# Splitting the first weight tile and turning the two token halves of four norms separately in a two-layer encoder kernel

## The chip, the cores and the metric

The kernel runs on one core of a Trainium2 chip. The metric is the device time of one execution in microseconds (us). The engines are named as in the profile: PE is TensorE, DVE is VectorE, ACT is ScalarE, POOL is GpSimd, SP is SyncE, which here issues the DMAs.

## What is computed

Two layers over 256 tokens of 1024 features. Each layer is a mixer (five groups of heads on one input projection, then an output projection) and a feed-forward part with product-key experts (PEER). Both begin with an RMS norm:

```python
def rmsnorm(x, g):
    xf = x.astype(jnp.float32)
    xf = xf * lax.rsqrt(jnp.mean(xf * xf, axis=-1, keepdims=True) + EPS)
    return xf.astype(x.dtype) * g

for l in range(DEPTH):
    xn = rmsnorm(x, norm_mix[l])
    proj = xn @ w_in[l]
    ...
    kv = rmsnorm(mem, mem_g) @ w_kv
    ...
    x = x + cat @ w_out[l]
    x = x + peer_ffn(rmsnorm(x, norm_ffn[l]), peer_wq[l], peer_subkeys[l], peer_u[l], peer_v[l])
```

mem is a second input of 256 rows of 1024 features; it feeds keys and values of one of the five groups.

## The kernel before

**Weights.** All weights come as a stream of 128 x 1024 tiles (class Stream). `fill` loads a tile w_raw by a DMA from SP (L70; three buffers) and splits it into w_hi, a rounded copy made by ACT (L82), and w_lo, the remainder made by DVE (L84), three buffers of each. A product is then three matmuls on a 128 x 128 block of weights: w_hi with the activations' high part (L240), w_hi with their low part (L241) and w_lo with the high part (L242). `out_t_job` runs them for the eight chunks of 128 features, each over all 256 tokens, into ps_mm; `pair_job` does so for two weight tiles in a row.

**Start.** The first products are those of mem with the four tiles of w_kv. `mem_load` brings mem in four pieces of two chunks each (L302) and splits each chunk into mh (ACT, L303) and ml (DVE, L304). Of the first two weight tiles the first is loaded ahead of the first memory piece and the second ahead of the second piece.

**Norms.** `rms_transposed` (L202 to L234) is called four times: for the mixer (into tile xs) and the feed-forward part (FFN; its scaled tokens lie in a tile named H) of either layer. The tokens lie on the partitions, in two halves of 128 (tt). Per half, ACT squares and sums (two instructions, L214), DVE makes the mean (L217), POOL the power -1/2 (L219), then DVE scales the first 512 features (L220) and ACT the others (L221). The matmuls need features on the partitions, so PE transposes (L227): a tile ps_t of PSUM takes two chunks of features with both halves, four transposes. ACT writes xh from it (L230, one instruction per chunk, 128 x 256), times the gain, and DVE writes xl (L231), which needs ps_t and xh. After the fourth chunk, `stream.release` lets the splitting of the next weights go on.

**Order.** The program is written as loops, but a scheduler of the framework sets the order of the instructions on each engine, by dependencies and priorities; `high_priority` surrounds the norms. On the chip each engine then runs its instructions in that order. In the mixer norms other work of the memory group is woven in: mm_vz (L478, ACT, from ps_v), rs_e (L364, ACT), ps_rb (L368, PE), mm_k (L417, DVE), mm_kz (L672, ACT). ps_t and ps_v share two buffers of PSUM there.

Of the kernel before, what the change touches and what calls it, by code (L numbers as in the profile page):

```python
# [10 lines left out]
F32 = mybir.dt.float32  # L11
# [4 lines left out]
AF = mybir.ActivationFunctionType  # L16
ALU = mybir.AluOpType
# [3 lines left out]
P = 128  # L21
T = 256
D = 1024
NC = D // P
# [6 lines left out]
AFTER = 3  # L31
MEM_CHUNK = 2
# [23 lines left out]
class Stream:  # L56


    def __init__(self, tc, raw_pool, hl_pool, sources, ahead, split_ahead):
        self.tc, self.nc, self.raw_pool, self.hl_pool, self.sources = tc, tc.nc, raw_pool, hl_pool, sources  # L60
        self.ahead, self.split_ahead = ahead, split_ahead
        self.raw, self.parts = {}, {}
        self.n_raw = self.n_parts = self.pos = 0
        self.limit = len(sources)
        self.after = ()

    def fill(self, upto=None):
        while self.n_raw < min(len(self.sources), self.pos + self.ahead, upto or len(self.sources)):
            t = self.raw_pool.tile([P, D], F32, name="w_raw")
            self.last_load = self.nc.sync.dma_start(t, self.sources[self.n_raw][0])  # L70
            self.raw[self.n_raw] = t
            self.n_raw += 1
        while self.n_parts < min(self.n_raw, self.pos + self.split_ahead, self.limit):
            r = self.raw.pop(self.n_parts)
            with ExitStack() as ctx:
                ctx.enter_context(self.tc.high_priority(SPLIT_AHEAD))
                for ins in self.after:
                    ctx.enter_context(self.tc.issue_after(ins.ins))
                self.after = ()
                hi = self.hl_pool.tile([P, D], F32R, name="w_hi")  # L80
                lo = self.hl_pool.tile([P, D], F32R, name="w_lo")
                self.nc.scalar.copy(hi, r)  # L82
                on_pool = self.sources[self.n_parts][1]
                (self.nc.gpsimd if on_pool else self.nc.vector).tensor_sub(lo, r, hi.bitcast(F32))  # L84
            self.parts[self.n_parts] = (hi, lo)
            self.n_parts += 1

    def release(self, after):

        self.limit, self.after = len(self.sources), after  # L90
# [46 lines left out]
def build(tc, x, mem, w_in, w_kv, w_out, wq, u_t, v_t, subk, pool_w, conv_pw, vec, dist, inv_count, ind, out, depth=2,  # L137
          dbg=None):
    nc = tc.nc
    V, A, G = nc.vector, nc.scalar, nc.gpsimd  # L140
# [14 lines left out]
    with (  # L155
# [9 lines left out]
        stream = Stream(tc, raw_pool, hl_pool, sources, 4, 3)  # L165
        ident = cp.tile([P, P], F32, name="ident")
# [23 lines left out]
        def vv(name, src=None):  # L190
            a, b = VEC[name]
            return (vecs if src is None else src)[:, a:b]
# [9 lines left out]
        def rms_transposed(pool, psum, src, xs, gain, hi, lo, in_hi=False):  # L202


            with tc.high_priority():
                for tt in range(2):
                    s = xs[:, tt, :]
                    ss = xp.tile([P, 2], F32, name="rn_ss", bufs=2)
                    for hf in range(2):
                        if in_hi:  # L210
                            junk = hi[:, 4 * tt + 2 * hf:4 * tt + 2 * hf + 2, :].rearrange("p c t -> p (c t)")
                        else:
                            junk = s[:, hf * 512:(hf + 1) * 512]
                        A.activation(junk, src[:, tt, hf * 512:(hf + 1) * 512], AF.Square, scale=1.0 / 32,  # L214
                                     accum_out=ss[:, hf:hf + 1])
                    ms = xp.tile([P, 1], F32, name="rn_ms", bufs=2)
                    V.tensor_scalar(ms, ss[:, 0:1], ss[:, 1:2], EPS, op0=ALU.add, op1=ALU.add)  # L217
                    rs = xp.tile([P, 1], F32, name="rn_rs", bufs=2)
                    pows.append(G.tensor_tensor(out=rs, in0=ms, in1=mhalf, op=ALU.pow))  # L219
                    V.tensor_scalar(s[:, 0:512], src[:, tt, 0:512], rs[:, 0:1], None, op0=ALU.mult)  # L220
                    A.activation(s[:, 512:], src[:, tt, 512:], AF.Identity, scale=rs[:, 0:1])  # L221
                for c in range(NC):
                    if c % 2 == 0:
                        ps = psum([P, 2, T], "ps_t")
                        for k in range(2):
                            for tt in range(2):
                                nc.tensor.transpose(ps[:, k, tt * P:(tt + 1) * P], xs[:, tt, (c + k) * P:(c + k + 1) * P],  # L227
                                                    ident)
                    pf = ps[:, c % 2, :]
                    a_ins = A.activation(hi[:, c, :], pf, AF.Identity, scale=gain[:, c:c + 1])  # L230
                    v_ins = V.scalar_tensor_tensor(lo[:, c, :], pf, gain[:, c:c + 1], hi[:, c, :].bitcast(F32),  # L231
                                                   op0=ALU.mult, op1=ALU.subtract)
                    if c == AFTER:
                        stream.release((a_ins, v_ins))  # L234

        def out_t_job(ps, hi, lo, xh, xl):

            for c in range(NC):
                wh, wl = hi[:, c * P:(c + 1) * P], lo[:, c * P:(c + 1) * P]
                nc.tensor.matmul(ps, wh, xh[:, c, :], start=(c == 0), stop=False)  # L240
                nc.tensor.matmul(ps, wh, xl[:, c, :], start=False, stop=False)  # L241
                nc.tensor.matmul(ps, wl, xh[:, c, :], start=False, stop=(c == NC - 1))  # L242
# [49 lines left out]
        def mem_load(mem_t, gains, weights=()):  # L292

            mh = xp.tile([P, NC, T], F32R, name="mh", tag="xh")
            ml = xp.tile([P, NC, T], F32R, name="ml", tag="xl")
            gain = vv("mem_norm", gains)
            with tc.high_priority() if not weights else nullcontext():
                for c in range(NC):
                    if c % MEM_CHUNK == 0:
                        if c // MEM_CHUNK in weights:  # L300
                            stream.fill(weights[c // MEM_CHUNK])
                        nc.sync.dma_start(mem_t[:, c:c + MEM_CHUNK, :], mem[:, c:c + MEM_CHUNK, :])  # L302
                    A.activation(mh[:, c, :], mem_t[:, c, :], AF.Identity, scale=gain[:, c:c + 1])  # L303
                    V.scalar_tensor_tensor(ml[:, c, :], mem_t[:, c, :], gain[:, c:c + 1], mh[:, c, :].bitcast(F32),  # L304
                                           op0=ALU.mult, op1=ALU.subtract)
            mem_parts[:] = [mh, ml]
# [779 lines left out]
```

## Time and profile before

| | us |
|---|---|
| runs shown | 2001.5, 2002.0, 2003.91 |
| median of the runs | 2002.0 |
| the profiled execution's own time | 2001.33 |
| its span in the trace | 1999.6 |
| PE busy in the span | 1964.6 (98%) |
| DVE busy | 1445.5 (72%) |
| ACT busy | 987.9 (49%) |

The span is the time from the first to the last instruction of the profiled execution; what the execution's own time has on top of it is start and end. Times in the trace count from the span's start. "Busy" sums the instructions' durations on an engine. The idle time before an instruction is shown in brackets with what released it: `[0.58 <-DVE xl L231]` means that the engine stood idle for 0.58 us until DVE's instruction on line 231, which writes xl, had ended.

### The profile page before, as it was taken

The numbers are of one execution on the slowest core, as the hardware profiler recorded it, in microseconds if no ns is written. First come the engines' busy times: TensorE is split into PE (matmuls) and PEld (weight loads), VectorE is DVE, ScalarE is ACT, GpSimd is POOL, SyncE is SP. The second block draws the span as 40 slices with busy tenths as digits, with TensorE's granted clock in tenths as the row PEclk, the third lists the DMA queues.
The fourth block names the chain that finished last, engine by engine and source line by source line (L and its number), as shares of the span: only waits on it lengthen the run. The fifth ranks groups of instructions, "written<-read, shape, count | busy, mean of one in ns | idle before, by whom it ended". The sixth has DMA issues, their size and how long they took to land.

```text
span 1999.6 us, 33683 instructions
## 1 busy us (share of the span) xinstructions
PE 1964.6 (98%) x13122; PEld 1809.9 (91%) x13122; DVE 1445.5 (72%) x2847; ACT 987.9 (49%) x1436; POOL 88.2 (4%) x141
## 2 busy tenths in 40 slices
PE   8999999999999999999999999999999999999999
PEld 7978999999999888888899789999999998888887
DVE  6976899788985655555578669987889755555555
ACT  6564455544444544444465645544444444444443
POOL 2310000000000000000023100000000000000000
PEclk9999999999999999999999999999999999999999
DMA  6314454434345555555553244554343455555554
GB/s 216 137 69 169 165 180 169 159 138 144 132 159 186 202 191 190 190 193 193 192 175 117 74 169 169 171 179 148 138 145 131 158 180 192 193 192 190 190 192 156
DMA packets 92769, 331.50 MB, mean 166 GB/s; under 512 B 10817, under 2 KB 11713, under 8 KB 92353
## 3 DMA queue, kind: packets, MB, share of 16 engines
q1 hardware_dynamic: 92608, 329.34, 48.3%
q8 instruction: 103, 1.69, 0.3%
q14 instruction: 58, 0.47, 0.1%
HBM read 328.25 MB, written 1.05 MB: 165 GB/s over the span
## 4 chain that ended last, share of the span: by engine, by line
PE 94%; DVE 3%; ACT 1%; issue 1%; DMA 0%; POOL 0%; SPq 0%; DVEq 0%; ACTq 0%; POOLq 0%
PE ps_mm L241 16%; PE ps_mm L240 16%; PE ps_mm L242 16%; PE acc_v L270 12%; PE acc_v L273 12%; PE acc_v L269 12%; PE ps_g L916 6%; PE ps_sc L804 1%; PE acc_o L269 1%; PE acc_o L273 1%; PE ps_o L496 1%; PE acc_o L270 1%; PE ps_ms L355 1%; DVE w_lo L84 1%; PE ps_t L227 0%
## 5 line engine op out<-in xcount | busy, mean ns | idle before, releaser
L84 DVE TENSOR_TENSOR w_lo<-w_raw,w_hi 128x1024 fp32r<-128x1024 f32 x612 | 748.6, 1223 | 421.2 <-ACT w_hi L82 420.9
L82 ACT CAST w_hi<-w_raw 128x1024 fp32r<-128x1024 f32 x612 | 641.6, 1049 | 760.3 <-PE ps_mm L241 499.4
L240 PE MATMUL ps_mm<-xh,w_hi 128*128 128x256 f32 x2624 | 752.5, 288 | 0.4 <-ACT xh L230 0.3
L241 PE MATMUL ps_mm<-xl,w_hi 128*128 128x256 f32 x2624 | 745.8, 285 | 0.1
L242 PE MATMUL ps_mm<-xh,w_lo 128*128 128x256 f32 x2624 | 744.4, 284 | 0.0
L241 PEld LDWEIGHTS ps_mm<-xl,w_hi 128*128 128x128 f32 x2624 | 505.5, 193 | 0.9 <-DVE xl L231 0.6
L240 PEld LDWEIGHTS ps_mm<-xh,w_hi 128*128 128x128 f32 x2624 | 504.3, 193 | 1.5 <-ACT xh L230 1.1
L242 PEld LDWEIGHTS ps_mm<-xh,w_lo 128*128 128x128 f32 x2624 | 504.8, 192 | 0.1
L270 PE MATMUL acc_v<-w_lo,a_hi 128*128 128x512 f32 x1016 | 316.3, 392 | 0.0
L273 PE MATMUL acc_v<-w_hi,a_lo 128*128 128x512 f32 x1016 | 315.2, 392 | 0.0
L269 PE MATMUL acc_v<-w_hi,a_hi 128*128 128x512 f32 x1016 | 273.9, 391 | 0.0
L273 PEld LDWEIGHTS acc_v<-w_hi,a_lo 128*128 128x128 f32 x1016 | 190.8, 188 | 42.4
L269 PEld LDWEIGHTS acc_v<-w_hi,a_hi 128*128 128x128 f32 x1016 | 190.8, 188 | 41.9
L270 PEld LDWEIGHTS acc_v<-w_lo,a_hi 128*128 128x128 f32 x1016 | 190.8, 188 | 40.7
L954 ACT CAST a_hi<-H 128x512 fp32r<-128x512 f32 x128 | 79.4, 622 | 153.7 <-PE acc_v L270 150.1
L956 DVE TENSOR_TENSOR a_lo<-H,a_hi 128x512 fp32r<-128x512 f32 x128 | 88.6, 693 | 77.7 <-ACT a_hi L954 77.7
L906 DVE TENSOR_SCALAR ag<-iota_f,i1T,gT 128x128 f32<-128x128 f32 x512 | 142.6, 342 | 0.0
L916 PE MATMUL ps_g<-ag,a 128*128 128x128 f32 x1024 | 125.1, 275 | 0.0
L916 PEld LDWEIGHTS ps_g<-ag,a 128*128 128x128 f32 x1024 | 120.2, 192 | 0.0
L901 DVE TENSOR_TENSOR a<-iota_f,i2T 128x1024 f32<-128x1024 f32 x64 | 77.8, 1218 | 1.7 <-PE ps_g L916 1.7
L921 DVE TENSOR_TENSOR H<-ps_g,H 128x184 f32<-128x184 f32 (+31 forms) x128 | 58.9, 464 | 1.2 <-ACT H L920 1.2
L943 ACT ACTIVATE H<-ps_mm 128x512 f32<-128x512 f32 (+31 forms) x106 | 49.4, 466 | 0.1
(242 smaller groups left out, 1296.7 us busy)
## 6 DMA issues: line engine op xcount, KB each, us to landing
w_raw<-u_t SPq DMA_DIRECT2D x256, 512.0 KB, 3.3
w_raw<-v_t SPq DMA_DIRECT2D x256, 512.0 KB, 3.4
w_raw<-w_in SPq DMA_DIRECT2D x40, 512.0 KB, 3.3
w_raw<-wq SPq DMA_DIRECT2D x32, 512.0 KB, 3.3
w_raw<-w_out SPq DMA_DIRECT2D x20, 512.0 KB, 3.2
w_raw<-w_kv SPq DMA_DIRECT2D x8, 512.0 KB, 3.4
H<-subk SPq DMA_DIRECT2D x2, 1024.0 KB, 4.9
mem_t<-mem SPq DMA_DIRECT2D x4, 256.0 KB, 6.2
```

The source lines that it names most:

```text
L82: self.nc.scalar.copy(hi, r)
L84: (self.nc.gpsimd if on_pool else self.nc.vector).tensor_sub(lo, r, hi.bitcast(F32))
L240: nc.tensor.matmul(ps, wh, xh[:, c, :], start=(c == 0), stop=False)
L241: nc.tensor.matmul(ps, wh, xl[:, c, :], start=False, stop=False)
L242: nc.tensor.matmul(ps, wl, xh[:, c, :], start=False, stop=(c == NC - 1))
L269: nc.tensor.matmul(accs[tt][hf], ah[:, s], hi[:, n], start=start, stop=False)
L270: nc.tensor.matmul(accs[tt][hf], ah[:, s], lo[:, n], start=False, stop=False)
L273: nc.tensor.matmul(accs[tt][hf], al[:, s], hi[:, n], start=False, stop=False)
L906: V.tensor_scalar(ag[:, t, :], iota_f, i1T[:, k:k + 1], gT[:, k:k + 1], op0=ALU.is_equal, op1=ALU.mult)
L916: nc.tensor.matmul(ps[:, t, :], a2[:, 4 * q + t, :], ag[:, 4 * q + t, :], start=True, stop=True)
L954: A.copy(ah, src)
L956: V.tensor_sub(al, src, ah.bitcast(F32))
```

## The change

**First weight tile.** It is loaded in two pieces of 512 columns, with the DMA of the first memory piece between them, and cast and subtracted in the same two pieces. All other tiles stay whole. SP's order is now first half, memory piece, second half, second weight tile, the other memory pieces; it was first tile, memory piece, second weight tile, the others. (The choice of POOL for w_lo, which no tile used, is dropped.)

**Norms.** The four squares come first. Both scalings of token half 0 go to DVE; of half 1, DVE does the first 512 features and ACT the others as before. A tile ps_t now takes four chunks of *one* token half. xh and xl are written per chunk and half, 128 x 128, 16 instructions on each engine instead of 8. The weights' splitting is released after chunk 3 of half 1.

```diff
     def fill(self, upto=None):
 ...
-            self.last_load = self.nc.sync.dma_start(t, self.sources[self.n_raw][0])
+            for k in self.pieces(self.n_raw):
+                self.last_load = self.nc.sync.dma_start(t[:, k], self.sources[self.n_raw][0][:, k])
+                if self.between:
+                    self.between.pop(0)()
 ...
-                self.nc.scalar.copy(hi, r)
-                on_pool = self.sources[self.n_parts][1]
-                (self.nc.gpsimd if on_pool else self.nc.vector).tensor_sub(lo, r, hi.bitcast(F32))
+                for k in self.pieces(self.n_parts):
+                    self.nc.scalar.copy(hi[:, k], r[:, k])
+                    self.nc.vector.tensor_sub(lo[:, k], r[:, k], hi[:, k].bitcast(F32))
 ...
+    def pieces(self, n):
+        return (slice(0, 512), slice(512, D)) if n == 0 else (slice(0, D),)
 ...
-                    V.tensor_scalar(s[:, 0:512], src[:, tt, 0:512], rs[:, 0:1], None, op0=ALU.mult)
-                    A.activation(s[:, 512:], src[:, tt, 512:], AF.Identity, scale=rs[:, 0:1])
-                for c in range(NC):
-                    if c % 2 == 0:
-                        ps = psum([P, 2, T], "ps_t")
-                        for k in range(2):
-                            for tt in range(2):
-                                nc.tensor.transpose(ps[:, k, tt * P:(tt + 1) * P], xs[:, tt, (c + k) * P:(c + k + 1) * P],
-                                                    ident)
-                    pf = ps[:, c % 2, :]
-                    a_ins = A.activation(hi[:, c, :], pf, AF.Identity, scale=gain[:, c:c + 1])
-                    v_ins = V.scalar_tensor_tensor(lo[:, c, :], pf, gain[:, c:c + 1], hi[:, c, :].bitcast(F32),
+                    rss.append(rs)
+                    if tt == 0:
+                        for hf in range(2):
+                            k = slice(hf * 512, (hf + 1) * 512)
+                            V.tensor_scalar(xs[:, 0, k], src[:, 0, k], rs[:, 0:1], None, op0=ALU.mult)
+                ps = {}
+                def turn(tt, c):
+                    if c % 4 == 0:
+                        ps[tt] = psum([P, 4, P], "ps_t")
+                        for k in range(4):
+                            nc.tensor.transpose(ps[tt][:, k, :], xs[:, tt, (c + k) * P:(c + k + 1) * P], ident)
+                    t = slice(tt * P, (tt + 1) * P)
+                    pf = ps[tt][:, c % 4, :]
+                    a_ins = A.activation(hi[:, c, t], pf, AF.Identity, scale=gain[:, c:c + 1])
+                    v_ins = V.scalar_tensor_tensor(lo[:, c, t], pf, gain[:, c:c + 1], hi[:, c, t].bitcast(F32),
                                                    op0=ALU.mult, op1=ALU.subtract)
-                    if c == AFTER:
+                    if tt and c == AFTER:
                         stream.release((a_ins, v_ins))
+                for c in range(4):
+                    turn(0, c)
+                V.tensor_scalar(xs[:, 1, 0:512], src[:, 1, 0:512], rss[1][:, 0:1], None, op0=ALU.mult)
+                A.activation(xs[:, 1, 512:], src[:, 1, 512:], AF.Identity, scale=rss[1][:, 0:1])
+                for c in range(4):
+                    turn(1, c)
+                for c in range(4, NC):
+                    turn(0, c)
+                    turn(1, c)
 ...
             with tc.high_priority() if not weights else nullcontext():
+                def load(c):
+                    nc.sync.dma_start(mem_t[:, c:c + MEM_CHUNK, :], mem[:, c:c + MEM_CHUNK, :])
                 for c in range(NC):
                     if c % MEM_CHUNK == 0:
+                        if c == 0 and weights:
+                            stream.between.append(lambda: load(0))
                         if c // MEM_CHUNK in weights:
                             stream.fill(weights[c // MEM_CHUNK])
-                        nc.sync.dma_start(mem_t[:, c:c + MEM_CHUNK, :], mem[:, c:c + MEM_CHUNK, :])
+                        if c or not weights:
+                            load(c)
```

How the scheduler orders it is seen in three places, all on ACT. A row is line, operation, output and inputs; tiles carry numbers, and a row that repeats is counted with x. What an instruction waits for stands in brackets: PE_49, DVE_49, Activation_49 and Pool_49 are the engines. A line of xh that waits for DVE waits for the xl that reads the same ps_t tile.

The mixer norm of layer 0, before (tiles ps_t 396, 405, 414 and 423 hold chunks 0-1, 2-3, 4-5 and 6-7):

```order
L230 ACTIVATE xh_376<-ps_t_396,vecs_123 128x256 [waits PE_49]
L478 COPY mm_vz_354<-ps_v_356 128x4x64 [waits PE_49,Pool_49]
L478 COPY mm_vz_354<-ps_v_356 128x4x64
L230 ACTIVATE xh_376<-ps_t_396,vecs_123 128x256 [waits DVE_49]
L230 ACTIVATE xh_376<-ps_t_405,vecs_123 128x256 [waits PE_49]
L230 ACTIVATE xh_376<-ps_t_414,vecs_123 128x256 [waits PE_49]
L230 ACTIVATE xh_376<-ps_t_405,vecs_123 128x256 [waits DVE_49]
L364 COPY rs_e2_280<-rs_m2_277 128x512 [waits Pool_49]
L230 ACTIVATE xh_376<-ps_t_414,vecs_123 128x256 [waits DVE_49]
L230 ACTIVATE xh_376<-ps_t_423,vecs_123 128x256 [waits PE_49]
L672 COPY mm_kz_266<-mm_k_287 64x2x256 [waits DVE_49]
L672 COPY mm_kz_266<-mm_k_287 64x2x256
```

and with the change (397 is half 0 and 412 half 1 of chunks 0-3, 425 and 432 the same of chunks 4-7):

```order
L242 ACTIVATE xh_379<-ps_t_397,vecs_123 128x128 [waits PE_49]
L506 COPY mm_vz_357<-ps_v_359 128x4x64 [waits PE_49,Pool_49]
L506 COPY mm_vz_357<-ps_v_359 128x4x64
L242 ACTIVATE xh_379<-ps_t_397,vecs_123 128x128 [waits DVE_49] x3
L242 ACTIVATE xh_379<-ps_t_412,vecs_123 128x128 [waits PE_49]
L242 ACTIVATE xh_379<-ps_t_412,vecs_123 128x128 [waits DVE_49]
L392 COPY rs_e2_283<-rs_m2_280 128x512 [waits Pool_49]
L242 ACTIVATE xh_379<-ps_t_412,vecs_123 128x128 [waits DVE_49]
L242 ACTIVATE xh_379<-ps_t_425,vecs_123 128x128 [waits PE_49]
L242 ACTIVATE xh_379<-ps_t_412,vecs_123 128x128 [waits DVE_49]
L242 ACTIVATE xh_379<-ps_t_425,vecs_123 128x128 [waits DVE_49] x3
L700 COPY mm_kz_269<-mm_k_290 64x2x256 [waits DVE_49]
```

Of half 1 the first piece (tile 412) stands behind three pieces of half 0, and mm_kz stands ahead of all pieces of tile 432. On PE the four transposes of tile 412 now stand ahead of the first matmul that reads xh.

The mixer norm of layer 1, before (10471, 10480, 10489 and 10498 hold two chunks each):

```order
L364 COPY rs_e2_10355<-rs_m2_10352 128x512 [waits Pool_49]
L230 ACTIVATE xh_10451<-ps_t_10471,vecs_9591 128x256 [waits PE_49]
L478 COPY mm_vz_10429<-ps_v_10431 128x4x64 [waits PE_49]
L478 COPY mm_vz_10429<-ps_v_10431 128x4x64
L230 ACTIVATE xh_10451<-ps_t_10471,vecs_9591 128x256 [waits DVE_49]
L230 ACTIVATE xh_10451<-ps_t_10480,vecs_9591 128x256 [waits PE_49]
L672 COPY mm_kz_10341<-mm_k_10362 64x2x256 [waits DVE_49]
L672 COPY mm_kz_10341<-mm_k_10362 64x2x256
L230 ACTIVATE xh_10451<-ps_t_10480,vecs_9591 128x256 [waits DVE_49]
L230 ACTIVATE xh_10451<-ps_t_10489,vecs_9591 128x256 [waits PE_49]
L230 ACTIVATE xh_10451<-ps_t_10489,vecs_9591 128x256 [waits DVE_49]
L230 ACTIVATE xh_10451<-ps_t_10498,vecs_9591 128x256 [waits PE_49]
```

and with the change (10504 is half 0 and 10519 half 1 of chunks 0-3, 10532 and 10539 the same of chunks 4-7):

```order
L242 ACTIVATE xh_10486<-ps_t_10504,vecs_9626 128x128 [waits PE_49]
L392 COPY rs_e2_10390<-rs_m2_10387 128x512 [waits Pool_49]
L506 COPY mm_vz_10464<-ps_v_10466 128x4x64 [waits PE_49]
L506 COPY mm_vz_10464<-ps_v_10466 128x4x64
L242 ACTIVATE xh_10486<-ps_t_10504,vecs_9626 128x128 [waits DVE_49] x2
L700 COPY mm_kz_10376<-mm_k_10397 64x2x256 [waits DVE_49]
L242 ACTIVATE xh_10486<-ps_t_10519,vecs_9626 128x128 [waits PE_49]
L700 COPY mm_kz_10376<-mm_k_10397 64x2x256
L242 ACTIVATE xh_10486<-ps_t_10504,vecs_9626 128x128 [waits DVE_49]
L242 ACTIVATE xh_10486<-ps_t_10519,vecs_9626 128x128 [waits DVE_49] x3
L242 ACTIVATE xh_10486<-ps_t_10532,vecs_9626 128x128 [waits PE_49]
L242 ACTIVATE xh_10486<-ps_t_10532,vecs_9626 128x128 [waits DVE_49] x2
```

rs_e moved behind the first piece, and the first piece of half 1 (10519) stands behind the first mm_kz, which waits for DVE (mm_k).

The FFN norm of layer 0, from the squares to the casts of the next weights, before (1868 and 1877 hold chunks 0-3):

```order
L214 ACTIVATE xh_1847,rn_ss_1850<-xt_73 128x512 [waits DVE_49] x2
L214 ACTIVATE xh_1847,rn_ss_1859<-xt_73 128x512 [waits DVE_49]
L221 ACTIVATE H_1849<-xt_73,rn_rs_1855 128x512 [waits PE_49,Activation_49,Pool_49]
L214 ACTIVATE xh_1847,rn_ss_1859<-xt_73 128x512 [waits DVE_49]
L221 ACTIVATE H_1849<-xt_73,rn_rs_1864 128x512 [waits Pool_49]
L230 ACTIVATE xh_1847<-ps_t_1868,vecs_123 128x256 [waits PE_49,Activation_49]
L230 ACTIVATE xh_1847<-ps_t_1877,vecs_123 128x256 [waits PE_49,Activation_49]
L230 ACTIVATE xh_1847<-ps_t_1868,vecs_123 128x256 [waits DVE_49]
L230 ACTIVATE xh_1847<-ps_t_1877,vecs_123 128x256 [waits DVE_49]
L82 CAST w_hi_1909<-w_raw_1790 128x1024 [waits DMAHW2_49]
```

and with the change (1885 is half 0, 1900 half 1 of chunks 0-3):

```order
L222 ACTIVATE xh_1866,rn_ss_1869<-xt_73 128x512 [waits DVE_49] x2
L222 ACTIVATE xh_1866,rn_ss_1878<-xt_73 128x512 [waits DVE_49] x2
L242 ACTIVATE xh_1866<-ps_t_1885,vecs_123 128x128 [waits PE_49,Activation_49]
L251 ACTIVATE H_1868<-xt_73,rn_rs_1883 128x512 [waits Pool_49]
L242 ACTIVATE xh_1866<-ps_t_1885,vecs_123 128x128 [waits DVE_49]
L242 ACTIVATE xh_1866<-ps_t_1900,vecs_123 128x128 [waits PE_49]
L242 ACTIVATE xh_1866<-ps_t_1885,vecs_123 128x128 [waits DVE_49]
L242 ACTIVATE xh_1866<-ps_t_1900,vecs_123 128x128 [waits DVE_49]
L242 ACTIVATE xh_1866<-ps_t_1885,vecs_123 128x128 [waits DVE_49]
L242 ACTIVATE xh_1866<-ps_t_1900,vecs_123 128x128 [waits DVE_49] x2
L87 CAST w_hi_1944<-w_raw_1809 128x1024 [waits DMAHW3_49]
```

One scaling left ACT, all squares stand ahead of it, and seven pieces of 128 x 128 stand between the scaling and the first cast where four instructions of 128 x 256 stood.

## Rows read from the trace of the kernel before

**Rows 1.** Page, part 4: the chain that ended last, by engine
```profile
PE 94%; DVE 3%; ACT 1%; issue 1%; DMA 0%; POOL 0%; SPq 0%; DVEq 0%; ACTq 0%; POOLq 0%
```

**Rows 2.** Waits of PE: engine, tile, line <- releaser: us in total, times, longest
```profile
PE ps_mm L240 <- ACT mh L303: 7.2, 2, 6.6
...
PE ps_t L227 <- DVE H L220: 3.5, 2, 1.8
```

**Rows 3.** Chain that ended last, first 11 us: start us, us, what
```profile
2.12 5.86 DMA w_raw<-w_kv
...
10.76 0.58 PE ps_mm L241
```

**Rows 4.** Groups by line and shape: xcount | busy us, mean ns | idle before
```profile
L230 ACT ACTIVATE xh<-ps_t,vecs 128x256 fp32r<-128x256 f32 x32 | 14.6, 474 | 7.8 <-PE ps_t L227 6.0 <-DVE xl L231 1.5
...
L920 ACT COPY H<-ps_g 128x256 f32<-128x256 f32 x4 | 1.5, 373 | 0.1
...
L920 ACT COPY H<-ps_g 128x128 f32<-128x128 f32 x4 | 1.1, 267 | 0.3
...
L231 DVE SCALAR_TENSOR_TENSOR xl<-ps_t,vecs,xh 128x256 fp32r<-128x256 f32 x32 | 14.9, 482 | 8.9 <-ACT xh L230 8.5
...
L921 DVE TENSOR_TENSOR H<-ps_g,H 128x256 f32<-128x256 f32 x4 | 1.7, 418 | 0.0
...
L921 DVE TENSOR_TENSOR H<-ps_g,H 128x176 f32<-128x176 f32 x4 | 1.4, 342 | 1.2 <-ACT H L920 1.2
```

**Rows 5.** Timeline, mixer norm, layer 0: start us, length, line, op [idle before <-releaser]
```profile
26.84 0.47 ACT L230 ACTIVATE xh<-ps_t,vecs 128x256 fp32r<-128x256 f32 x1 [0.70 <-PE ps_t L227]
...
27.22 0.65 ACT L478 COPY mm_vz<-ps_v 128x256 f32<-128x256 f32 x2
...
27.78 0.49 PE L240 MATMUL ps_mm<-xh,w_hi 128*128 128x256 f32 x2
...
35.14 0.39 PE L241 MATMUL ps_mm<-xl,w_hi 128*128 128x256 f32 x1
```

**Rows 6.** Timeline, mixer norm of layer 1
```profile
1016.15 0.60 PE L227 MATMUL ps_t<-ident,xs 128*128 128x128 f32 x4
...
1016.47 0.62 ACT L364 COPY rs_e<-rs_m 128x512 f32<-128x512 f32 x1 [0.26 <-POOL rs_m L359]
...
1017.56 0.48 PE L240 MATMUL ps_mm<-xh,w_hi 128*128 128x256 f32 x2
...
1017.90 0.74 DVE L417 SCALAR_TENSOR_TENSOR mm_k<-hn_x,vecs,ps_rb 128x512 f32<-128x512 f32 x1
...
1019.12 1.24 ACT L672 COPY mm_kz<-mm_k 64x512 f32<-64x512 f32 x2
...
1021.80 0.86 ACT L230 ACTIVATE xh<-ps_t,vecs 128x256 fp32r<-128x256 f32 x2 [0.58 <-DVE xl L231]
...
1024.87 0.28 PE L241 MATMUL ps_mm<-xl,w_hi 128*128 128x256 f32 x1
```

**Rows 7.** Timeline, FFN norm of layer 0
```profile
164.59 0.72 ACT L221 ACTIVATE H<-xt,rn_rs 128x512 f32<-128x512 f32 x1
...
165.22 0.61 ACT L214 ACTIVATE xh<-xt 128x512 fp32r<-128x512 f32 x1
...
168.56 0.39 PE L240 MATMUL ps_mm<-xh,w_hi 128*128 128x256 f32 x1 [0.30 <-ACT xh L230]
...
169.82 1.98 ACT L82 CAST w_hi<-w_raw 128x1024 fp32r<-128x1024 f32 x2
...
173.54 0.28 PE L242 MATMUL ps_mm<-xh,w_lo 128*128 128x256 f32 x1
```

**Rows 8.** Windows us: length, busy of each engine (xcount), granted clock, DMA share, GB/s
```profile
24.50:26.00 1.50, 0.00 (x0) 0.00 (x0) 1.43 (x4) 1.50 (x3) 1.50 (x2) 1.00 0.83 243
...
169.00:173.00 4.00, 3.89 (x18) 3.49 (x19) 3.40 (x6) 3.12 (x5) 0.00 (x0) 0.57 0.00 0
...
1159.00:1166.00 7.00, 6.84 (x30) 5.94 (x29) 5.50 (x9) 5.28 (x10) 0.00 (x0) 0.51 0.27 93
```

More of the change, by code (lines that the diff above doesn't have):

```diff
@@ L65, in __init__ @@
         self.after = ()
+        self.between = []
     def fill(self, upto=None):
@@ L205, in rms_transposed @@
             with tc.high_priority():
+                rss = []
                 for tt in range(2):
-                    s = xs[:, tt, :]
                     ss = xp.tile([P, 2], F32, name="rn_ss", bufs=2)
@@ L212, in rms_transposed @@
                         else:
-                            junk = s[:, hf * 512:(hf + 1) * 512]
+                            junk = xs[:, tt, hf * 512:(hf + 1) * 512]
                         A.activation(junk, src[:, tt, hf * 512:(hf + 1) * 512], AF.Square, scale=1.0 / 32,
```

## Prediction

> **What bounds the kernel now.** The page comes first: 94% of the chain that ended last is TensorE's own work [rows 1]. Nothing is gained by making another engine faster on the average; only places where TensorE stands still can be won, and every new place where it stands still is added to the time. The next view is therefore the list of TensorE's waits, and the reader should look there at the lines that the change touches. Two of the longest are at such lines: the first matmul waits for the first memory piece (7.2 us in two waits), and in the two FFN norms the transposes wait for the scaled half H, 3.5 us in two waits [rows 2]. The chain of the first 11 us says what the start really hangs on: not the first piece but the *second* weight tile, whose load takes from 2.12 to 7.98; its cast and the memory chunks behind it give the matmul at 10.76 from which TensorE runs through [rows 3]. Last, the four norms are read in the timeline, since there TensorE gets its operand xh and xl one chunk at a time. The link there is serial: ACT writes xh of a chunk, DVE reads the same PSUM tile for xl, and only then does ACT begin the next chunk of that tile; a pair of xh is held back for 0.58 us with DVE's xl named as what released it [rows 6].
>
> The profiled execution took 2001.33 us, 0.7 us under the median of 2002.0 us of the runs. The sum below is made against 2001.33. About 0.2%, 4 us, is what a measurement of this kernel can tell from no change.
>
> **The start.** One DMA issue more stands on SP, and the cast and subtraction of tile one are in two pieces. The bytes ahead of the second weight tile are the same (first tile and first memory piece), and the chain [rows 3] goes through that tile's load. What comes earlier is the first matmul, which is followed by a wait for the second piece anyway. I take 0, with -0.5 (an earlier start lets the first matmuls clear the way) and +0.5 us (the added SP issue delays the second tile by about its own length) as ends.
>
> **The price of a piece.** Each norm made 8 xh and 8 xl of 256 columns; it now makes 16 and 16 of 128. The trace has no such pieces. For ACT, reads from PSUM cost 373 ns for 256 columns and 267 for 128, so 128 columns less save 106 ns; from the 474 ns of xh this leaves 0.37 us [rows 4]. For DVE, 418 ns at 256 and 342 at 176 are 0.95 ns a column; the 482 ns of xl become 0.36 us [rows 4]. Ends: 0.27 (the plain copy of 128) and 0.47 (no saving) for ACT, 0.30 and 0.48 for DVE. A link, xh then xl and a gap of about 0.04 us on either side, was 0.474 + 0.482 + 0.08 = 1.04 us for a whole chunk and is p = 0.37 + 0.36 + 0.08 = 0.81 us for half a chunk (0.65 to 1.04). A chunk now needs two. Where pieces of different tiles alternate on ACT, one starts about 0.28 us after the other, since records of ACT overlap by some 0.1 us (the xh at 26.84 with 0.47 us is followed at 27.22 [rows 5]).
>
> The Trainium skill, "PSUM — Partial Sum Buffer", section "PSUM bank collisions raise a hardware error", says that ScalarE and VectorE must not touch one bank in the same partitions together, even at other columns; it speaks against a change that puts four pieces into one bank. The trace agrees, with the 0.58 us wait above [rows 6]; were pieces of one bank free to overlap, a link would shrink to DVE's pace of about 0.4 us, and the third rival would hold. The skill's "VectorE: DVE Perf Modes", section "The TRN2 errata", gives 172 + columns cycles (ScalarE, 1.2 GHz) and 120 + columns (VectorE, 0.96 GHz) for PSUM sources, an estimate of 0.25 and 0.26 us for 128 columns; it makes 0.36 and 0.39 of what is 0.474 and 0.482 here, so the rows decide. By it p would be 0.59, and the sixteen links of the two mixer norms below would take 16 x 0.22 = 3.5 us less (the third rival).
>
> **Mixer norm, layer 0.** A matmul needs xh of a chunk for all 256 tokens, so the first now waits for a piece of half 0 and one of half 1. In the new order ACT makes piece (half 0, chunk 0), two mm_vz, three more pieces of half 0, and only then (1,0). Piece (0,0) starts some 0.2 us after the 26.84 of now, since two more matmuls stand ahead of its transposes (a pair takes 0.49 us where one takes 0.39 [rows 5]); mm_vz comes 0.28 later and takes 0.65 us [rows 5], so (0,1) starts at 28.0; two links and one alternation later, at 28.0 + 1.62 + 0.28 = 29.9, (1,0) starts, and the first L240 comes at 30.3 where it now has its operand at 27.8 [rows 5]: +2.5. From there the chain, not TensorE, sets the end: link to (1,1), rs_e (0.53 us to the next start), (1,2), (0,4), link to (1,3), (0,5), two links to (0,7), mm_kz (1.24 us [rows 6] and a gap), three links from (1,4) to (1,7): 29.9 + 0.81 + 0.28 + 0.53 + 0.81 + 0.28 + 1.62 + 0.28 + 1.28 + 2.43 = 38.2. Then xh and xl of the last piece, 0.77 us: the last chunk's L241 at 39.0 instead of 35.14 [rows 5], **+3.9 us**. Nine links are in it: at p = 0.65 it is +2.5, at 1.04 +5.9.
>
> **Mixer norm, layer 1.** Transposes end at 1016.75 [rows 6]; (0,0) starts at 1016.8, and rs_e, now behind it, 0.28 later (before: 1016.47). mm_vz ends at 1018.25, (0,1) follows; its xl at 1018.66 is ahead of mm_k (0.74 us [rows 6]) in DVE's queue, so mm_k ends at 1019.7. The first mm_kz (half of 1.24 us [rows 6]) waits for that, and (1,0) stands behind it in ACT's queue: 1020.35, first L240 at 1020.75 where it now has its operand at 1017.8: +2.9. The second mm_kz follows; then (0,3) at 1021.26, (1,1) 0.28 later, two links to (1,3), 0.28, two links to (0,6), 0.28 to (1,4), one link from (0,6) to (0,7), 0.28, two links to (1,7) at 1027.8, and 0.77: 1028.5 for the last L241 instead of 1024.87 [rows 6], **+3.7 us** (+2.5 to +5.2).
>
> **FFN norm, layer 0.** Doing all squares first takes ACT's scaling at 164.59 from before the fourth square at 165.22 [rows 7]. The square can start when the third ends, an estimate of 0.47 us earlier, and mean and pow follow; the first L240 gains about 0.26, since it now needs one more piece. But ACT does eight pieces, in turn from two tiles at DVE's pace of about 0.38 us, before it casts the next weights; the first comes before the pow, the others after it; the casts move from 169.82 [rows 7] to about 170.55, DVE's w_lo behind them likewise, and the L242 of the second weight, at 173.54 now [rows 7], has to wait until some 174.0: **+0.4 us**. In layer 1 nine pieces stand ahead of the casts, one of them linked: **+0.6**. Ends for each: -0.3 (only the earlier pow) and +1.5 (p at 1.04). The squares stay where they were, behind the last additions of out_projection.
>
> **Sum.** 0 + 3.9 + 3.7 + 0.4 + 0.6 = +8.6: 2001.33 + 8.6 = **2009.9 us**. With every low end it is 2001.33 - 0.5 + 2.5 + 2.5 - 0.6 = 2005.2, with every high end 2015.9. All later work is TensorE-bound, so a delay is carried to the end.
>
> **Rivals.**
> - *The clock stays up in the FFN norms; not slower.* After the norms' idle time TensorE was granted 0.57 of its clock for 4 us in layer 0 and 0.51 for 7 us in layer 1, the lower of its two levels (1.2 instead of 2.4 GHz) [rows 8]: 4 x 0.43 + 7 x 0.49 = 5.1 us. The transposes of half 0 now come while half 1 still waits for its pow, so TensorE has eight transposes' work more evenly within that idle time. If that keeps the clock up in both, and pieces cost the low end, the time is 2005.2 - 5.1 = 2000.1. Against it: four transposes are 0.6 us [rows 6], little beside two waits of 1.8 us before them and after [rows 2]. It decides from the point at which both stretches keep the clock.
> - *The clock falls in the mixer norms.* TensorE now stands still for 2.5 to 2.9 us more; in 24.5 to 26 it stood still for 1.5 us and the granted clock was 1.00 [rows 8]. If it falls as in the FFN norms, each costs 1.7 to 3.4 us: about 2014.
> - *The pieces are cheap or the links overlap.* The delay is then the wait for the first chunk alone: +2.1 and +2.5, FFN at -0.3 to +0.2: about 2006.
> - *The start gains nothing, or the whole change does less than it says:* the first half of this is in the sum; the norms' order is moved on all engines, so nothing remains of the second.
>
> **How the numbers follow.** The sum at about its size has 0.5, cheap pieces 0.25 (half of that under 2006, within 0.2%), the falling clock 0.13, the clock kept up 0.12 (half of it faster by over 0.2% if the start gains too). Scheduling elsewhere has moved too (the attention's background work about 1100 to 1130), which I put at 1 us either way. This gives faster 0.06, same 0.22, slower 0.72, and a range from 2002.5 to 2014.
>
> **What would show it.** Right: xh at some 370 ns and xl at 360; the first L240 after each mixer norm 2.5 to 2.9 us after its place now, with ACT xh as its releaser in TensorE's waits, and new waits of L240 and L241 on xh and xl in the course of the chunks; the two ACT stretches ahead of the casts longer by 0.7 us; the L241 from which TensorE runs through at about 10.8 as now. Wrong: granted clock 1.00 where it was 0.57 and 0.51, xh pieces of one tile that start without waiting for xl, or TensorE's total wait in the mixer norms under 3 us.

## The result, and the profile after

The changed kernel takes 2015.2 us (median of 6 runs, 2013.92 to 2019.27) against 2003.38 us for the kernel before in the same comparison (6 runs, 2001.5 to 2006.21): ratio 1.0061, 95% interval 1.0048 to 1.0074, 12 us slower. The forecast was 2009.9 us with a range from 2002.5 to 2014: the direction was right, the size too small. Two things must be kept apart in that difference. The profiled execution of before (2001.33 us) lies low among the runs of its kernel, which in later comparisons went from 2000.07 to 2007.93, so the spans of the two traces differ by 13.9 us where the medians differ by 11.8; and the traces of the two profiled executions, spans 1999.6 and 2013.5 us, show in which stage the time went.

For a table by stage, the starts of all 13122 matmuls of each trace were put in order; the number says how much later the matmul of the same rank starts than in the trace of before. Within a stage the order differs in places, so a rank need not be the same product there.

| behind | before, us | change: later by | in this stage | forecast |
|---|---|---|---|---|
| the first memory products | 24.0 | 1.02 | +1.0 | 0 |
| mixer norm, layer 0 | 49.9 | 7.37 | +6.35 | +3.9 |
| mixer work of layer 0 | 160.6 | 7.89 | +0.5 | |
| FFN norm, layer 0 | 184.9 | 8.41 | +0.5 | +0.4 |
| mixer norm, layer 1 | 1027.7 | 12.99 | +4.6 | +3.7 |
| mixer work of layer 1 | 1154.5 | 13.79 | +0.8 | |
| FFN norm, layer 1 | 1182.0 | 14.00 | +0.2 | +0.6 |

Two lines from the list of TensorE's waits before:

```profile
PE ps_v L475 <- DVE mm_vT L679: 2.3, 2, 1.5
...
PE ps_mm L240 <- ACT xh L230: 0.3, 1, 0.3
```

The same list of the changed kernel (L262 to L264 are the matmuls that were L240 to L242, L239 the transposes, L242 and L243 the pieces of xh and xl):

```profile
PE ps_mm L262 <- ACT mh L331: 8.3, 2, 5.6
...
PE ps_mm L262 <- ACT xh L242: 4.4, 6, 1.6
PE ps_v L503 <- DVE mm_vT L707: 4.0, 2, 3.3
...
PE ps_t L239 <- DVE H L250: 2.6, 2, 1.3
```

The waits on xh have grown from 0.3 to 4.4 us, and that on H is shorter than the 3.5 us of [rows 2], both as forecast. What was not forecast is the line on mm_vT: its longest wait, ahead of the mixer norm of layer 0, has grown from 1.5 to 3.3 us. The pieces themselves, in the groups by shape, are as estimated (0.37 and 0.36 us):

```profile
L242 ACT ACTIVATE xh<-ps_t,vecs 128x128 fp32r<-128x128 f32 x64 | 21.8, 366 | 17.1 <-DVE xl L243 11.4 <-PE ps_t L239 5.5
...
L243 DVE SCALAR_TENSOR_TENSOR xl<-ps_t,vecs,xh 128x128 fp32r<-128x128 f32 x64 | 20.9, 348 | 19.5 <-ACT xh L242 19.4
```

ACT and DVE now wait for each other for 11.4 and 19.4 us in all; [rows 4] had 1.5 and 8.5. The timeline ahead of the mixer norm of layer 0, before:

```profile
24.29 0.37 ACT L378 COPY mem_r<-ps_rb 128x256 f32<-128x256 f32 x1 [0.93 <-PE ps_rb L368]
24.55 1.05 ACT L82 CAST w_hi<-w_raw 128x1024 fp32r<-128x1024 f32 x1
...
24.69 0.69 DVE L410 TENSOR_TENSOR hn_x<-ps_mm,mem_r 128x512 f32<-128x512 f32 x1
25.30 0.68 DVE L679 TENSOR_TENSOR mm_vT<-ps_mm,mem_r 128x512 f32<-128x512 f32 x1
25.89 1.22 DVE L84 TENSOR_TENSOR w_lo<-w_raw,w_hi 128x1024 fp32r<-128x1024 f32 x1
...
26.04 0.33 PE L475 MATMUL ps_v<-ident,mm_vT 128*128 128x128 f32 x1 [1.55 <-DVE mm_vT L679]
```

and with the change, from there to the end of the norm:

```profile
25.10 1.04 ACT L87 CAST w_hi<-w_raw 128x1024 fp32r<-128x1024 f32 x1 [1.39 <-PE ps_mm L263]
26.05 0.36 ACT L406 COPY mem_r<-ps_rb 128x256 f32<-128x256 f32 x1
28.04 0.63 ACT L440 ACTIVATE hn_sq<-hn_x 128x512 f32<-128x512 f32 x1 [1.62 <-DVE hn_x L438]
29.46 0.37 ACT L242 ACTIVATE xh<-ps_t,vecs 128x128 fp32r<-128x128 f32 x1 [0.79 <-PE ps_t L239]
...
38.09 1.25 ACT L700 COPY mm_kz<-mm_k 64x512 f32<-64x512 f32 x2 [1.04 <-DVE mm_k L445]
...
40.93 0.37 ACT L242 ACTIVATE xh<-ps_t,vecs 128x128 fp32r<-128x128 f32 x1 [0.42 <-DVE xl L243]
41.72 0.37 ACT L242 ACTIVATE xh<-ps_t,vecs 128x128 fp32r<-128x128 f32 x1 [0.42 <-DVE xl L243]
...
26.18 1.22 DVE L88 TENSOR_TENSOR w_lo<-w_raw,w_hi 128x1024 fp32r<-128x1024 f32 x1 [1.65 <-ACT w_hi L87]
27.32 0.68 DVE L438 TENSOR_TENSOR hn_x<-ps_mm,mem_r 128x512 f32<-128x512 f32 x1
...
28.65 0.33 PE L503 MATMUL ps_v<-ident,mm_vT 128*128 128x128 f32 x1 [3.25 <-DVE mm_vT L707]
...
32.63 0.79 PE L262 MATMUL ps_mm<-xh,w_hi 128*128 128x256 f32 x2 [0.98 <-ACT xh L242]
...
42.55 0.35 PE L263 MATMUL ps_mm<-xl,w_hi 128*128 128x256 f32 x1
```

With the change the cast of the seventh weight tile stands ahead of mem_r on ACT, and its subtraction w_lo ahead of hn_x on DVE. Before, the cast came behind mem_r and the subtraction behind mm_vT. So mem_r, hn_x, mm_vT, ps_v and the first transposes, which hang on each other, all come late: the first xh piece at 29.46 instead of 26.84 [rows 5]. Granted clock in windows (the figure behind the five engines' busy times), first the kernel before, then the changed kernel:

```profile
28.00:38.00 10.00, 9.99 (x84) 9.70 (x84) 5.30 (x10) 5.69 (x11) 1.83 (x2) 1.00 0.30 105
```

```profile
28.00:38.00 10.00, 8.37 (x47) 7.88 (x48) 5.03 (x16) 5.78 (x16) 3.12 (x4) 0.66 0.26 91
1030.00:1034.00 4.00, 3.84 (x20) 3.80 (x20) 2.19 (x7) 1.87 (x6) 0.00 (x0) 0.58 0.02 4
176.00:181.00 5.00, 4.83 (x22) 4.33 (x22) 3.48 (x8) 4.15 (x10) 0.00 (x0) 0.66 0.03 8
1173.00:1178.00 5.00, 4.46 (x20) 3.93 (x20) 3.03 (x8) 3.82 (x10) 0.00 (x0) 0.66 0.04 18
```

Behind the 3.25 us of idle time the clock is at its lower level for much of the norm, and it falls in layer 1's mixer norm also, where it was 1.00 before. In the FFN norm of layer 0 it falls as it did before: it costs 5 x 0.34 = 1.7 us, and cost 4 x 0.43 = 1.7 in [rows 8]. In that of layer 1 it costs less, 5 x 0.34 = 1.7 us instead of 7 x 0.49 = 3.4. Last, the start, in the chain that ended last:

```profile
2.59 6.09 DMA w_raw<-w_kv
...
11.46 0.58 PE ps_mm L263
```

The second weight tile is issued 0.47 us later (one more issue on SP) and takes 0.23 us longer to land than in [rows 3]; the matmul from which TensorE runs through comes 0.7 us later.

### The profile page after: what moved, and what is told of

It reads as the page before. It is cut to its first block, busy times and chain, and to the rows that moved or that the text cites. A ratio compares the mean times of both kernels' runs of the same rounds, so it can differ in the third digit from the quotient of the medians.

```text
span 2013.5 us, 33735 instructions
## 1 busy us (share of the span) xinstructions
PE 1970.9 (98%) x13122; PEld 1814.9 (90%) x13122; DVE 1452.7 (72%) x2884; ACT 992.8 (49%) x1465; POOL 88.5 (4%) x141
## 3 DMA queue, kind: packets, MB, share of 16 engines
HBM read 328.25 MB, written 1.05 MB: 164 GB/s over the span
## 4 chain that ended last, share of the span: by engine, by line
PE 91%; DVE 6%; ACT 1%; issue 1%; DMA 0%; SPq 0%; POOL 0%; DVEq 0%; ACTq 0%; POOLq 0%
PE ps_mm L263 15%; PE ps_mm L262 15%; PE ps_mm L264 15%; PE acc_v L292 12%; PE acc_v L295 12%; PE acc_v L291 12%; PE ps_g L944 6%; DVE w_lo L88 1%; DVE cv_ac L468 1%; PE ps_sc L832 1%; DVE cv_ac L462 1%; PE acc_o L295 1%; PE acc_o L291 1%; PE acc_o L292 1%; PE ps_o L524 0%
## 5 line engine op out<-in xcount | busy, mean ns | idle before, releaser
L88 DVE TENSOR_TENSOR w_lo<-w_raw,w_hi 128x1024 fp32r<-128x1024 f32 (+1 forms) x613 | 748.2, 1221 | 420.0 <-ACT w_hi L87 417.3
L87 ACT CAST w_hi<-w_raw 128x1024 fp32r<-128x1024 f32 (+1 forms) x613 | 641.8, 1047 | 757.1 <-PE ps_mm L263 497.7
L262 PE MATMUL ps_mm<-xh,w_hi 128*128 128x256 f32 x2624 | 753.0, 288 | 4.6 <-ACT xh L242 4.4
L263 PE MATMUL ps_mm<-xl,w_hi 128*128 128x256 f32 x2624 | 747.4, 285 | 0.0
L264 PE MATMUL ps_mm<-xh,w_lo 128*128 128x256 f32 x2624 | 745.4, 285 | 0.9 <-DVE w_lo L88 0.9
L262 PEld LDWEIGHTS ps_mm<-xh,w_hi 128*128 128x128 f32 x2624 | 504.8, 193 | 7.2 <-ACT xh L242 6.3
L263 PEld LDWEIGHTS ps_mm<-xl,w_hi 128*128 128x128 f32 x2624 | 506.7, 193 | 1.2 <-DVE xl L243 0.6
L264 PEld LDWEIGHTS ps_mm<-xh,w_lo 128*128 128x128 f32 x2624 | 506.2, 193 | 1.4 <-DVE w_lo L88 1.2
```

The costliest lines, as they stand in the source:

```text
L87: self.nc.scalar.copy(hi[:, k], r[:, k])
L88: self.nc.vector.tensor_sub(lo[:, k], r[:, k], hi[:, k].bitcast(F32))
```

## The experiments

Ten experiments, each measured against runs of the kernel before on the same chip. "Seventh tile" is the one whose cast slipped ahead of mem_r. The edits are shown in part. What a norm adds is read as in the table by stage, from one trace of each kernel.

**start_alone**: only the split tile, the norms as before.

```diff
+            for k in self.pieces(self.n_raw):
+                self.last_load = self.nc.sync.dma_start(t[:, k], self.sources[self.n_raw][0][:, k])
+                if self.between:
+                    self.between.pop(0)()
```

> Only the split first weight tile, with the first memory piece between its halves; the norms are as before. Theory A (each part of the change adds its own delay, the start by one DMA issue ahead of the second weight tile): second tile lands 0.7 us later, the matmul from which TensorE runs through comes at 11.46 instead of 10.76, and the span is 0.7 to 1.0 us longer than before (about 2000.5). Rival B (the start is free, all comes from the norms): span within 0.2 us of before; a gain would need the run-through matmul before 10.76.

Ratio 1.0002 (0.9992 to 1.0011). Its trace has the later start: the load of the second tile takes from 2.59 to 9.00, the matmuls between 10 and 14 us start 1.0 us late, and those behind the first memory products still 0.5. Mixer norm 0 adds 1.6 us in this trace, at a granted clock of 0.83 in 28 to 38; mixer_old_ffn_new, which has the same start and the same mixer norm, adds nothing there. The runs do not show a loss: neither gain nor loss above 0.1%. (The profiled execution, 2007.62 us, is the longest of its ten; see the last section.)

**norms_alone**: rms_transposed as in the change, loads and splitting of the weights as before.

```diff
+                rss = []
...
-                        ps = psum([P, 2, T], "ps_t")
+                        ps[tt] = psum([P, 4, P], "ps_t")
```

> The norms of the change, the start as before. Theory A: the span is that of the change less the start's 0.7 to 1.0 us, about 2012.7, so 13 us over before. Rival C (the late start is what pushes the layer-0 mixer norm into the slow order and the low clock): under 2009, the first xh piece at most 0.5 us later than in the kernel before.

Ratio 1.0050 (1.0033 to 1.0067). The wait for mm_vT is 3.3 us and the mixer norm of layer 0 adds 6.4 us here too, without the late start: rival C is out. The norms carry it.

**squares_first**: new order of squares and scalings, old tiles and whole pieces.

```diff
+                    rss.append(rs)
+                    if tt == 0:
+                        for hf in range(2):
+                            k = slice(hf * 512, (hf + 1) * 512)
+                            V.tensor_scalar(xs[:, 0, k], src[:, 0, k], rs[:, 0:1], None, op0=ALU.mult)
```

> The four squares first and both scalings of half 0 on DVE, but tiles of two chunks with both halves and pieces of 256 columns as before. Theory A: the squares-first order puts a cast ahead of mem_r on ACT and a w_lo ahead of hn_x on DVE, TensorE's wait for mm_vT grows from 1.5 to about 3 us, +1.6 us there, with -0.3 us in each FFN norm: span +0.5 to +2 (2000.1 to 2001.6), more if the clock falls in the layer-0 mixer norm (up to +2 more). Rival B (only the half pieces cost): -0.6 us, 1999.0.

Ratio 1.0045 (1.0028 to 1.0062), more than any theory said. Its waits and the same window as above:

```profile
PE ps_v L480 <- DVE mm_vT L684: 4.0, 2, 3.3
```

```profile
28.00:38.00 10.00, 10.00 (x62) 10.00 (x60) 3.88 (x9) 5.46 (x12) 2.24 (x3) 0.66 0.25 74
```

The 3.3 us wait and the lower clock come with the squares' order alone; mixer norm 0 adds 4.6 us and mixer norm 1 another 1.8, there at a granted clock of 1.00. A further 4.4 us are not the change's: they lie between 120 and 154 us of the trace of before, where a ps_rb waits 2.3 us for an rs_e and the changed kernel loses nothing.

**halves_old_squares**: new tiles and half pieces, squares and scalings as before.

```diff
-                        ps = psum([P, 2, T], "ps_t")
+                        ps[tt] = psum([P, 4, P], "ps_t")
```

> Tiles of four chunks of one half and pieces of 128 columns, squares and scalings per half as before. Theory A: no cast ahead of mem_r, wait for mm_vT 1.5 us as before, but the chain of half pieces in both mixer norms: +3.5 to +4 us each, +0.5 us in each FFN norm: span +8 to +9 (2007.6 to 2008.6), TensorE waiting for xh. Rival D (the moved cast and the low clock behind it are the larger part, half pieces are mostly hidden): +2 to +4, 2001.6 to 2003.6.

Ratio 1.0059 (1.0039 to 1.0079). The wait for mm_vT is 1.5 us as before, the clock 1.00 in 28 to 38, and still mixer norm 0 adds 2.2 us and mixer norm 1 another 2.2, not the 3.5 to 4 that I expected. These 4.4 us lie between rival D (2 to 4 in all) and theory A. FFN norm 0 adds 1.3; the rest is again elsewhere (2.6 us in layer 0's attention, 2.1 in layer 1's).

**pieces_only**: old tiles, old order, each piece made in two.

```diff
-                    pf = ps[:, c % 2, :]
-                    a_ins = A.activation(hi[:, c, :], pf, AF.Identity, scale=gain[:, c:c + 1])
+                    for tt in range(2):
+                        t = slice(tt * P, (tt + 1) * P)
+                        pf = ps[:, c % 2, t]
+                        a_ins = A.activation(hi[:, c, t], pf, AF.Identity, scale=gain[:, c:c + 1])
```

> The kernel before with each 128x256 piece of xh and xl made in two of 128x128, in the old tiles and the old order of chunks. Theory A (a serial link of 0.79 us per half piece instead of 1.04 per chunk): +1.5 to +2.5 us in each mixer norm, +0.5 in each FFN norm, 4 to 6 us over before at the same mean clock. Rival E (the cost comes from the halves' order, since the first matmul needs a piece of both halves; small pieces are hidden behind the matmuls): under 2 us over before.

Ratio 1.0053 (1.0038 to 1.0069). TensorE waits 6.5 us for xh, where the list of the kernel before had 0.3 us:

```profile
PE ps_mm L242 <- ACT xh L232: 6.5, 8, 1.7
```

Mixer norm 0 adds 2.6 us and mixer norm 1 3.5: rival E is out, halving the pieces costs even in the order of before. FFN norm 0 adds 1.7. Some 4.5 us more fall on layer 0's attention, where a ps_rb waits 2.1 us for an rs_e that stands behind a cast on ACT.

**after_hold6**: the change, with the seventh tile held back.

```diff
+            if not l:
+                stream.limit = 6
             pair_job(mh, ml, mem_k, B)
             pair_job(mh, ml, mem_v, B)
+            if not l:
+                stream.release((marks["mem_r"], marks["vT"]))
+                stream.fill()
```

> The change, with the seventh weight tile's cast queued behind mem_r on ACT and its subtraction behind mm_vT on DVE, which is where both stood before the change. Theory A (squares first let them slip ahead, and the idle time this makes brings the clock down in the layer-0 mixer norm): TensorE's wait for mm_vT 3.3 us becomes 1.5 to 2.0, the first xh piece comes at about 27.9 instead of 29.46, the granted clock stays 1.00 in 28 to 38, span 2 to 4.5 us under the change's 2013.5. Rival D (the chain of half pieces alone sets the end of the norm): at most 1 us under it.

Ratio 1.0031 (1.0018 to 1.0044) instead of 1.0061: part of the loss is back, half by the ratios, less by the medians (2012.65 against 2003.59 us). Timeline on ACT, and the window:

```profile
25.21 0.37 ACT L406 COPY mem_r<-ps_rb 128x256 f32<-128x256 f32 x1 [1.47 <-PE ps_rb L396]
25.48 1.05 ACT L87 CAST w_hi<-w_raw 128x1024 fp32r<-128x1024 f32 x1
...
27.76 0.37 ACT L242 ACTIVATE xh<-ps_t,vecs 128x128 fp32r<-128x128 f32 x1 [0.70 <-PE ps_t L239]
```

```profile
28.00:38.00 10.00, 8.62 (x65) 7.65 (x64) 5.57 (x18) 7.35 (x21) 3.12 (x4) 1.00 0.31 107
```

The first piece comes at 27.76, the wait for mm_vT is 1.8 us, the clock stays at its upper level, and mixer norm 0 adds 2.55 us instead of 6.35. One cast and its subtraction out of their place, with the clock and the order of the pieces that follow, are worth 3.8 us in that norm. The profiled span, 2011.9 us, is only 1.6 us under that of the change, where 2 to 4.5 were expected: this trace loses 1.6 us in layer 0's mixer work and 2.2 in layer 1's, against 0.5 and 0.8 in the trace of the change.

**squares_first_hold6**: squares first in all norms, whole pieces, seventh tile held.

```diff
+                stream.release((marks["mem_r"], marks["vT"]))
```

> Squares first with whole pieces in all four norms, and the seventh weight tile's cast and subtraction queued behind mem_r and mm_vT. Theory A (in the squares-first kernel the moved cast alone delays the layer-0 mixer norm, and the idle time brings its clock down): wait for mm_vT 1.5 to 2.0 us instead of 3.3, granted clock 1.00 up to 40 us, matmuls behind that norm at most 0.5 us later than in the kernel before (squares first alone: 4.1 us later); the time 3 us or more under squares first alone. Rival H (the delay comes from the scalings' place, not from the cast): 2 us or more later behind that norm still, time within 1 us of squares first alone.

Ratio 1.0008 (0.9997 to 1.0019), against 1.0045 without the hold. The wait for mm_vT is 1.8 us, the clock 1.00 in 28 to 38, and the norm of layer 0 adds 0.1 us instead of 4.6; rival H is out. The kernel's order differs elsewhere from that of squares_first too, so not all of the 0.37% belongs to the hold.

**mixer_old_ffn_new**: the change without its mixer norms.

```diff
-            rms_transposed(mp, psum, xt, xs, vv("norm_mix"), xh, xl)
+            rms_old(mp, psum, xt, xs, vv("norm_mix"), xh, xl)
```

> The change in the FFN norms and at the start alone; the two mixer norms as before. Theory A (the mixer norms carry most of it): +0.5 to +1 in each FFN norm and up to +1 at the start, span within 3 us of before at the same mean clock, time 2003 to 2006. Rival F (the FFN norms' loss brings the lower clock and is larger than the norms' own delay): 2008 or more.

Ratio 0.9999 (0.9990 to 1.0009). The start and the FFN norms together cost nothing that the runs show, so the mixer norms carry the result. In the trace the FFN norms add 1.2 and 1.7 us all the same, more than in the changed kernel (0.5 and 0.2). In layer 1 the lower clock goes with that: it costs 10 x 0.31 = 3.1 us in 1160 to 1170 of this trace and 1.7 in the changed kernel's.

**ffn_squares_first**: the kernel before, with squares first in the FFN norms alone. It was measured twice.

```diff
-            rms_transposed(pp, psum, xt, xs, vv("norm_ffn"), xh, xl, True)
+            rms_squares_first(pp, psum, xt, xs, vv("norm_ffn"), xh, xl, True)
```

> The kernel before, with the squares first and both scalings of half 0 on DVE in the two FFN norms only; whole pieces, old tiles, mixer norms and start untouched. Theory A (the earlier pow is worth its 0.47 us where nothing is added): the first L240 of each FFN norm 0.3 to 0.5 us earlier, time 0.6 to 1.0 us under before, not told from it in the runs. Rival G (the scheduler's other choices behind the norm take it back): 0 to +3 us.

> The same kernel as ffn_squares_first once more, for a narrower interval: its first comparison gave 0.9987 (0.9978 to 0.9996) of before, while the traces of both have the same span. If the FFN norms' earlier pow is all there is, the ratio is 0.9993 to 1.0; if it is real as measured, again under 0.999.

Ratios 0.9987 (0.9978 to 0.9996) and 0.9994 (0.9985 to 1.0003). It is faster than the changed kernel, and the only one whose ratio lay under 1 with its whole interval once; the second measurement does not confirm that by itself. In its trace

```profile
PE ps_t L266 <- DVE H L259: 2.6, 2, 1.3
```

the wait for H falls from 3.5 us [rows 2] to 2.6, which is the 0.4 us per norm that the earlier power is worth; the second trace has 2.6 too. The shorter wait is shown. A gain in time is not: behind the two norms the matmuls gain 0.35 and 0.25 us in the first trace, and in the second they lose 0.3 and gain 1.5.

## Why the prediction was wrong in size

**Right: the price of a piece, and the length of the chain.** Pieces took 366 and 348 ns where 0.37 and 0.36 us were forecast, and a serial link 0.79 us (from 40.93 to 41.72 in the trace) where p was 0.81. From the first piece to the first matmul of layer 0's mixer norm the forecast had 30.3 - 27.04 = 3.3 us, the trace 32.63 - 29.46 = 3.2. In layer 1, with the 8.42 us that had come before, the first piece was due at 1016.8 + 8.42 = 1025.22 and came at 1025.21. The last chunk's L263 was due at 1028.5 + 8.42 = 1036.92 and came at 1037.79, 0.9 us later, which is the whole miss of that norm (4.6 instead of 3.7). The chain as forecast has no wait for transposes; in the trace ACT waits for those of tile 10532, which fall into the stretch at the lower clock:

```profile
1034.60 0.62 ACT L242 ACTIVATE xh<-ps_t,vecs 128x128 fp32r<-128x128 f32 x2 [1.05 <-PE ps_t L239]
```

(One reading was off and touches no sum: the operand of layer 1's first matmul was there at 1017.56 [rows 6], not at 1017.8, so that matmul was due 3.2 us later, not 2.9.)

**Wrong: "Piece (0,0) starts some 0.2 us after the 26.84 of now".** It came 2.62 us later, and this is the step that failed. Of these, 0.9 are the start and the order of the memory products; 1.7 are the growth of the wait for mm_vT from 1.55 to 3.25, with the cast and the subtraction of the seventh tile ahead of mem_r and hn_x. I followed the order from the first xh on and took everything ahead of it as unmoved; yet the order of ACT does show a cast ahead of mem_r. squares_first and halves_old_squares show which half of the change moves it (the squares), after_hold6 and squares_first_hold6 that its place is the cause (waits of 1.8 us with it put back). Why the scheduler moves the cast when the squares come first, the runs do not show.

**The second rival came on top.** It was given a chance of 0.13, and its idle time was "2.5 to 2.9 us more". In layer 0 the clock fell behind a wait of 3.25 us in the three kernels that have it (the change, norms_alone, squares_first: granted clock 0.66 in 28 to 38) and not in the others, whose wait is 1.5 to 1.8 (1.00); start_alone with 1.9 us lies between (0.83). In layer 1 it fell behind shorter waits: 0.78, 0.64 and 1.57 us between 1023 and 1029. At the lower level TensorE's work takes nearly twice as long (four transposes 1.05 to 1.11 us instead of 0.60), ps_rb comes late, mm_k behind it, and mm_kz makes ACT wait 1.04 us: the norm's chain, forecast at 39.0 - 27.04 = 12.0 us, took 42.55 - 29.46 = 13.1. That wait is not the clock's alone: halves_old_squares, at 1.00, has a wait of 0.81 us ahead of mm_kz. With these two steps the sum for layer 0 closes: 3.9 + 2.4 for the first piece + 1.1 for the chain = 7.4 us, which is the 7.37 that the table has behind that norm.

**Half pieces cost less, alone, than the sum said.** Where the cast was kept in place, mixer norm 0 lost 2.2 to 2.55 us, not 3.9. The order of the pieces is another one in those kernels (mm_kz stands earlier among them), and the forecast had worked through that of the changed kernel; how much of the difference is the order was not tried. In mixer norm 1 the halves alone add 2.2 us and the squares' order alone 1.8, both at a clock of 1.00; together they add 4.3 to 4.6 in the three kernels that have both, all at a lower mean clock (0.76 to 0.88 in the 14 us of that norm).

**"The start: I take 0" was outside its own ends in the trace** (+0.7 against 0.5) and within them in the runs (start_alone). The step that one more issue "delays the second tile by about its own length" was right for 0.47 us; the further 0.23 is the load itself.

**The FFN norms**: +0.5 and +0.2 instead of +0.4 and +0.6; the gain of 0.26 to the first matmul was seen as 7.89 - 7.61 = 0.28 (176.17 instead of 168.56, less what had come before). The first rival, a clock that stays up in both, did not happen; the smaller loss of clock in layer 1, 1.7 us instead of 3.4, is a part of it, and it came by luck: mixer_old_ffn_new, with the same FFN norms and a loss of 3.1 us there, adds 1.7 instead of 0.2. (The 1.8 us wait of [rows 2] stands once in each FFN norm; the wait ahead of the first transposes is 1.2 us.)

**The base of the sum** was a low execution: 2001.33 against a median of 2003.4 in 6 and 21 runs. The step "0.7 us under the median" rested on three runs. With 2003.4 as base the same sum gives 2012.0. The range, too, was narrower than the sum's own ends: these reached 2015.9, and the 2015.2 measured lie within them but outside the range to 2014.

## What to carry to other kernels

Where a scheduler sets the order, a change to one block can move work *ahead* of that block too: compare the order from the last place that is the same on every engine, and price each thing that has slipped in between, also one cast. Sharing the reading of a PSUM tile between two engines is here a serial chain per tile; halving the pieces takes 0.79 us twice where it was about 1.04 once (the sum from [rows 4]), and all five kernels with half pieces in the mixer norms lost 2.2 us or more in each of them. Test the parts of a change apart: here one part (squares first) cost 4.6 and 1.8 us in the two mixer norms and shortened a wait in the FFN norms.

## What the hardware showed that was not expected

The granted clock falls at other places in other executions of the same kernel. The two profiled executions of ffn_squares_first, on two chips, same windows, spans 1999.6 and 2002.4 us; first the one, then the other:

```profile
118.00:124.00 6.00, 5.13 (x26) 4.34 (x27) 5.86 (x16) 5.20 (x14) 0.70 (x1) 1.00 0.01 1
129.00:133.00 4.00, 4.00 (x26) 3.45 (x25) 3.82 (x13) 3.32 (x9) 0.00 (x0) 1.00 0.00 0
```

```profile
118.00:124.00 6.00, 4.74 (x16) 3.94 (x17) 5.41 (x15) 5.20 (x13) 0.69 (x1) 0.72 0.01 1
129.00:133.00 4.00, 4.00 (x12) 3.15 (x11) 3.13 (x10) 2.49 (x9) 0.42 (x1) 0.57 0.00 0
```

The attention work there leaves TensorE short gaps, and whether the clock falls there differs between the two; the spread of some 6 us between runs of one kernel goes with the clock: of 13 runs of before in one comparison, on one chip, the fastest, 2000.94 us, had a mean granted clock of 0.994, the slowest, 2006.73 us, 0.990. The Trainium skill, "TensorE: Matmul & The Clock Gate", section "Part 1: The HAM clock gate (the "warmup" mystery)", says that what the gate looks at runs free of the kernel, so that the same kernel meets it at another phase. The two traces (1.00 and 0.72) fit this, but no run here shows the phase. A difference of 2 us between two single traces therefore says nothing by itself, while a wait that recurs in three kernels' traces (the 3.3 us for mm_vT) does.
